# Queue order at stage borders, preparation transfers on GpSimd's queue, and a state-space stage written in a fixed order

## The chip, the cores and the metric

The kernel runs on one core of a Trainium2 chip. The metric is the device time of one execution in microseconds; the time shown for a kernel is the median of its runs. The core has TensorE (PE, matrix products; PEld are its weight loads), VectorE (DVE), ScalarE (ACT), GpSimd (POOL) and SyncE (SP). Each engine executes its instructions in the order in which they stand in its program; transfers (DMA) are issued from a queue of SP, ACT or POOL, and the issue itself waits its turn in that engine's program.

## What is computed

One decoding step of two layers for 512 prompt and 64 sample positions (576 columns together), all in float32:

```python
# layer 0: gated spatial MLP and differential attention, one output projection, then a SwiGLU feed-forward
a   = up * spatial_gate(vp, sgu_w, sgu_b)
b   = diff_head_out(diff_attn(q, k, v, lam), subln)
x1  = x  + concat(a, b) @ w_out_even
x2  = x1 + (silu(gate) * up) @ w_ffn_out          # gate, up = split(rmsnorm(x1) @ w_ffn_in), 22 blocks of 128
# layer 1: S5, 64 groups of 16 channels, one complex state of 64 each
s   = associative_scan(a_bar, b_bar @ rmsnorm(x2)) + a_cum * s0
y   = Re(c @ s) + d * u
z   = gelu(y) @ w_glu + b_glu
x3  = x2 + z[:, :1024] * sigmoid(z[:, 1024:])
x4  = x3 + swiglu(rmsnorm(x3))
out = rmsnorm(x4)                                  # and the new cache rows and the last states
```

## The kernel before

Activations are kept transposed, 128 channels by 576 columns, eight such tiles for the 1024 channels. A float32 product is made of three products in a shorter format: the weight is split into `wh` (a cast on ACT, L260) and `wl` (the rest, on DVE, L263), the activation into `hi` (ACT, L227 or L230) and `lo` (DVE, L228 or L231), and PE adds hi·wh, lo·wh and hi·wl (L278), 288 columns at a time. A *unit* is one output tile of 128 channels: `Stream` loads the raw weight (L245, on SP's queue, two buffers that hold two units each), splits it at most two units ahead, and runs `unit_mm` (L269), either half of the columns after the other, or, where `kmajor` is set, k by k with both halves in turn. Each half ends in an `evac` on DVE.

The stages in order of time: input projection; attention with side work; the output projection into `x1` (`ev_o`, L1040); feed-forward 0 (`push_ffn`, in four parts of 6, 6, 6 and 4 blocks, each with its gate and up units and then eight down units); the S5 stage; the gated units (`ev_z1`); feed-forward 1; the last norm. `s5_prep` (L1256 on) works beside feed-forward 0 in small portions: for every k of 0 to 7 (eight groups each) it makes the matrices Gk, Fk and Tk of the state-space model with DVE, ACT and PE, stores them to scratch tensors in DRAM (dG, dF, and dZ from which dL is copied with a shift), and the S5 stage loads them back (`s5_load`, L1563).

A norm needs the sum of squares over 1024 channels. `Stat.add` (L985) squares each new tile on ACT (L987, L990), adds it into `acc` on POOL (L998), and `mm` (L1001) sums `acc` and the last square over the partitions on PE (`ssq`, L1007).

For each k the S5 stage does: U scaled by the norm (L1639, DVE), `vp` = U·Gk (L1645, PE), rotation, W and scan on DVE (L1666, L1667, L1682, L1683), a second rotation and the states `X` (L1692, DVE), `yp` = Tk·U + Fk·X (L1702, L1708, PE), copies on ACT, transposes (L1722, PE), gelu and split. The letters of `SORD` give the order in which the functions for k, k+1 and so on are called.

What sets the order: a scheduler orders the instructions of each engine with estimates of its own, except where the text pins them (`keep`) or, in the changed kernel, inside `tc.manual_schedule()`, where the program's order stands. Small tiles come from rings: 44 buffers for `blk`, 19 for `ablk`, 5 in the pool `op`; four PSUM banks each for `mbank` and `bank`.

## Time and profile before

| | us |
|---|---|
| median of 3 runs | 1432.93 (1428.97 to 1440.73) |
| the profiled execution | 1436.56 |
| its span, first to last instruction | 1434.86 |
| mean granted TensorE clock | 0.986 |
| PE busy | 1384.8 |

The difference of execution and span, 1.7 us, lies outside the instructions. PE is busy 97% of the span; the rest is to be read as stretches in which PE has nothing to do, and besides these there are stretches in which its clock was granted at half. The trace shows two levels, 1.0 (2.4 GHz) and 0.5 (1.2 GHz).

### The profile page before, as it was taken

How to read it: one execution, taken by the hardware profiler on the slowest of the kernel's cores; microseconds unless marked ns; L12 is line 12 of the kernel's file. 1: busy time of each engine (PE TensorE's matmuls, PEld its weight loads, DVE VectorE, ACT ScalarE, POOL GpSimd, SP SyncE). 2: the span in 40 equal slices, each digit the busy share in tenths (PEclk: the TensorE clock that was granted, in tenths of full speed). 3: DMA queues.
4: the chain of work that ended last, by engine and by line, in shares of the span. 5: the costliest groups of instructions: out<-in, count | busy, mean ns of one | idle time of the engine just before them, and what ended most of it. 6: DMA issues, size and time to landing. Idle time of an engine off the chain costs nothing. (4 is left out here: it accounts for less than half of the span.)

```text
span 1434.9 us, 27625 instructions
## 1 busy us (share of the span) xinstructions
PE 1384.8 (97%) x11382; PEld 1317.7 (92%) x11382; DVE 840.3 (59%) x1979; ACT 482.8 (34%) x866; POOL 182.3 (13%) x220
## 2 busy tenths in 40 slices
PE   7999999989999999999999979999999999999997
PEld 6888887769999999999998968999999999999997
DVE  5544567567599545987964487544444444444455
ACT  4233465433332123333322535433221221222234
POOL 2453553431000000000000200010000000000002
PEclk9999999999999999999999979999999999999999
DMA  8565653453322433555456684233223322322411
GB/s 240 166 199 179 202 178 104 133 180 122 89 80 87 133 89 80 152 145 147 146 141 179 201 238 134 68 89 89 62 72 103 89 74 74 89 81 75 110 59 67
DMA packets 223557, 177.37 MB, mean 124 GB/s; under 512 B 34060, under 2 KB 199752, under 8 KB 223432
## 3 DMA queue, kind: packets, MB, share of 16 engines
q1 hardware_dynamic: 206312, 136.01, 32.9%
q0 software_dynamic: 10880, 35.66, 8.2%
q10 hardware_dynamic: 6240, 3.93, 0.9%
q8 instruction: 90, 1.47, 0.4%
q14 instruction: 35, 0.29, 0.1%
HBM read 154.24 MB, written 25.53 MB: 125 GB/s over the span
## 5 line engine op out<-in xcount | busy, mean ns | idle before, releaser
L278 PE MATMUL acc<-hi,wh 128*128 128x288 f32 x2432 | 724.3, 298 | 6.0 <-ACT wh L260 3.1
L278 PE MATMUL acc<-hi,wl 128*128 128x288 f32 x2432 | 720.1, 296 | 1.5 <-DVE wl L263 1.5
L278 PE MATMUL acc<-lo,wh 128*128 128x288 f32 x2432 | 719.4, 296 | 0.0
L278 PEld LDWEIGHTS acc<-hi,wh 128*128 128x128 f32 x2432 | 458.7, 189 | 12.6 <-ACT hi L227 4.5
L278 PEld LDWEIGHTS acc<-hi,wl 128*128 128x128 f32 x2432 | 458.9, 189 | 3.7 <-DVE wl L263 2.4
L278 PEld LDWEIGHTS acc<-lo,wh 128*128 128x128 f32 x2432 | 459.1, 189 | 0.9 <-issue 0.8
L260 ACT CAST wh<-raw 128x1024 fp32r<-128x1024 f32 (+2 forms) x196 | 185.0, 945 | 592.9 <-PE acc L278 410.8
L263 DVE TENSOR_TENSOR wl<-raw,wh 128x1024 fp32r<-128x1024 f32 (+2 forms) x195 | 214.1, 1099 | 56.1 <-ACT wh L260 54.4
L1121 DVE TENSOR_TENSOR tu<-acc,rb 128x288 f32<-128x288 f32 x88 | 40.1, 455 | 124.6 <-PE acc L278 124.5
L278 PE MATMUL acc<-gxh,wh 128*128 128x288 f32 x320 | 100.2, 316 | 0.9 <-DVE proj L372 0.9
L1111 DVE TENSOR_TENSOR tg<-acc,rb 128x288 f32<-128x288 f32 x88 | 39.9, 455 | 97.1 <-PE acc L278 96.1
L278 PE MATMUL acc<-gxl,wh 128*128 128x288 f32 x320 | 96.4, 302 | 0.0
L278 PE MATMUL acc<-gxh,wl 128*128 128x288 f32 x320 | 95.5, 301 | 0.6 <-DVE wl L263 0.6
L998 POOL TENSOR_TENSOR acc<-acc,sq 128x576 f32<-128x576 f32 x18 | 26.8, 1488 | 480.9 <-ACT sq L990 480.9
L1131 DVE TENSOR_TENSOR x<-acc,x 128x288 f32<-128x288 f32 x96 | 43.6, 456 | 73.5 <-PE acc L278 73.1
L731 POOL DMA_INDIRECT pg<-in_cache_v_dram,pidx x64 | 65.0, 1016 | 82.9 <-PE so L853 49.4
L731 POOL DMA_INDIRECT pg<-in_cache_k_dram,pidx x64 | 64.1, 1001 | 71.8 <-PE ktp L786 36.4
L278 PEld LDWEIGHTS acc<-gxh,wh 128*128 128x128 f32 x320 | 60.9, 191 | 8.7 <-issue 8.0
L1841 POOL TENSOR_TENSOR sq<-sq,sq 128x288 f32<-128x288 f32 x12 | 9.6, 802 | 431.2 <-ACT sq L1837 431.2
L278 PEld LDWEIGHTS acc<-gxh,wl 128*128 128x128 f32 x320 | 60.7, 190 | 1.7 <-DVE wl L263 0.8
L278 PEld LDWEIGHTS acc<-gxl,wh 128*128 128x128 f32 x320 | 61.1, 191 | 1.0 <-issue 0.7
L227 ACT CAST hi<-tu 128x576 fp32r<-128x576 f32 x44 | 29.8, 677 | 41.9 <-DVE tu L1123 41.9
(441 smaller groups left out, 1474.0 us busy)
## 6 DMA issues: line engine op xcount, KB each, us to landing
raw<-in_w_ffn_in_dram SPq DMA_DIRECT2D x88, 512.0 KB
raw<-in_w_ffn_out_dram SPq DMA_DIRECT2D x24, 768.0 KB
raw<-in_w_in_even_dram SPq DMA_DIRECT2D x10, 1024.0 KB
...
```

The costliest lines, as they stand in the source:

```text
L227: A.copy(hi, src)
L260: c = A.copy(hi[:, 0:nk], src)
L263: c = (lo_eng or V).tensor_tensor(lo[:, 0:nk], src, f32(hi[:, 0:nk]), op=ALU.subtract)
L278: PE.matmul(pts[hf], lhsT=w[:, k, :], rhs=x[:, c0:c1], start=(k == 0 and wi == 0), stop=(k == nk - 1 and wi == 2))
L731: G.indirect_dma_start(out=t, out_offset=None, in_=src, in_offset=bass.IndirectOffsetOnAxis(ap=pidx[:, 8 * b + j:8 * b + j + 1], axis=0))
L998: G.tensor_tensor(self.acc[:, 0:NT], self.acc[:, 0:NT], q, op=ALU.add)
L1111: V.tensor_tensor(half(t, hf), pt, half(stat.need(), hf), op=ALU.mult)
L1121: V.tensor_tensor(half(t, hf), pt, half(stat.need(), hf), op=ALU.mult)
L1131: V.tensor_tensor(half(nxt[m], hf), pt, half(cur[m], hf), op=ALU.add)
L1841: G.tensor_tensor(acc[h], acc[h], q, op=ALU.add)
```

## The change

- `Stat.add` adds on DVE instead of POOL, and the `ssq` matmuls of `acc` move from the last `add` to the start of `steps`, which the driver calls later. In `ev_o` and `ev_z1` the split of a tile stands before its `add`, so ACT makes `hi` before the square.
- In `push_ffn` the first down unit of a part runs k by k.
- All transfers of `s5_prep` move to POOL's queue: those of ACT (ast, s0st, zz, dq) and those of SP (braw, cst, dF, dG, dZ, dL). dF gets another layout: two stores of 256 pieces of 512 B a half, and two loads of 128 partitions instead of four of 64.
- `s5_load` of k = 0 and 1 goes to POOL's queue too; the tables come out of the pool `op`; the order is Gk, tables, Tk, Fk.
- The S5 stage stands in `tc.manual_schedule()`, in the order 'LVDrxsRcoyg'. Both `vp` are in `bank`. X is written 64 wide and the last state copied out by ACT (L1694 goes); both W additions come before the two scans; two gated units instead of one run inside the stage.

```diff
-SORD = 'LrxsRVDcyog'
+SORD = 'LVDrxsRcoyg'
...
-        def add(self, x, pre=True):
+        def add(self, x):
...
-                    if pre:
-                        self.mm(self.acc, True)
...
-                    G.tensor_tensor(self.acc[:, 0:NT], self.acc[:, 0:NT], q, op=ALU.add)
+                    V.tensor_tensor(self.acc[:, 0:NT], self.acc[:, 0:NT], q, op=ALU.add)
...
         def steps(self):
             yield
+            self.mm(self.acc, True)
             r = self.tm()
...
+            gx1[m] = split(x1[m], g_ffn0[:, m:m + 1])
             st1.add(x1[m])
-            gx1[m] = split(x1[m], g_ffn0[:, m:m + 1])
...
-                    W.push(loads[mp], nf, hs, [ev(2 * mp), ev(2 * mp + 1)])
+                    W.push(loads[mp], nf, hs, [ev(2 * mp), ev(2 * mp + 1)], kmajor=(mp == 0))
...
-    dF = [dp.tile([P, 8, P], F32, name=f"dF{k}") for k in range(KD)]
+    dF = [dp.tile([2, 64, 2, 512], F32, name=f"dF{k}") for k in range(KD)]
...
-                SP.dma_start(out=br[64 * c:64 * c + 64], in_=I[key][0, 32 * hf:32 * hf + 32].rearrange("g p c -> p g c"))
+                G.dma_start(out=br[64 * c:64 * c + 64], in_=I[key][0, 32 * hf:32 * hf + 32].rearrange("g p c -> p g c"))
...
-                SP.dma_start(out=dL[k].rearrange("(c t) g n -> t c g n", t=8)[t],
+                G.dma_start(out=dL[k].rearrange("(c t) g n -> t c g n", t=8)[t],
                              in_=dZ[k][:, :, 16 * (7 - t):16 * (7 - t) + P].rearrange("g c n -> c g n"))
...
     def s5_load(k):
+        Q = G if k < 2 else SP
...
-        vp = [mbank("vp"), bank("vp")]
+        vp = [bank("vp"), bank("vp")]
...
-            V.tensor_tensor(x2k[k][:, c, :, 1:64], t1[:, c, :, 0:63], t2[:, 1 - c, :, 0:63], op=ALU.subtract if c == 0 else ALU.add)
-        for c in range(2):
-            V.tensor_tensor(fin2[:, c, 4 * k:4 * k + 4], t1[:, c, :, 63], t2[:, 1 - c, :, 63], op=ALU.subtract if c == 0 else ALU.add)
+            V.tensor_tensor(x2k[k][:, c, :, 1:65], t1[:, c], t2[:, 1 - c], op=ALU.subtract if c == 0 else ALU.add)
+        A.copy(fin2[:, :, 4 * k:4 * k + 4], x2k[k][:, :, :, 64])
+        A.copy(x2k[k][:, :, :, 64:72], s0[:, :, 4 * k:4 * k + 4, :])
...
-    glu0 = unit_mm(u0["hl"], u0["xs"], u0["nk"], u0["evac"], True, 1)
+    glus = [unit_mm(u["hl"], u["xs"], u["nk"], u["evac"], True, 1) for u in W.q[W.done:W.done + 2]]
...
-    for i in range(KD + 4):
-        for c in SORD:
-            f, d = steps[c]
-            on(f, i + d)
+    with tc.manual_schedule():
+        ru_mm(st2.last, False)
+        ru = rstd_fast(ru["ps"][:, 0:NCH], NCH, DM)
+        for k in range(VA):
+            on(s5_v, k)
+        on(s5_d0, 0)
+        for i in range(KD + 3):
+            for c in SORD:
+                f, d = steps[c]
+                on(f, i + d)
```

First place, the end of the output projection. DVE before: the two halves of `x1`, the next weight's rest, and the tile's `lo`, once per unit.

```order
L1047 TENSOR_TENSOR x_4626<-acc_4613,xa_4265 128x36x8
L1047 TENSOR_TENSOR x_4626<-acc_4628,xa_4265 128x36x8
L263 TENSOR_TENSOR wl_4650<-raw_4527,wh_4649 128x512
L231 SCALAR_TENSOR_TENSOR lo_4646<-x_4626,gvec,hi_4645 128x576
L1047 TENSOR_TENSOR x_4666<-acc_4653,xa_4333 128x36x8
L1047 TENSOR_TENSOR x_4666<-acc_4668,xa_4333 128x36x8
```

DVE after, the same tiles (the names' numbers differ a little, and so do the lines):

```order
L1046 TENSOR_TENSOR x_4626<-acc_4613,xa_4265 128x36x8
L1046 TENSOR_TENSOR x_4626<-acc_4628,xa_4265 128x36x8
L263 TENSOR_TENSOR wl_4650<-raw_4527,wh_4649 128x512
L231 SCALAR_TENSOR_TENSOR lo_4643<-x_4626,gvec,hi_4642 128x576
L996 TENSOR_TENSOR acc_316<-acc_316,sq_4646 128x576
L1046 TENSOR_TENSOR x_4666<-acc_4653,xa_4333 128x36x8
L1046 TENSOR_TENSOR x_4666<-acc_4668,xa_4333 128x36x8
```

The addition into `acc` has come onto DVE as a fifth instruction per tile, behind `lo`. PE at the same place, before, from the last matmul of the output projection on (acc_4704) into the first gate unit (acc_4791):

```order
L278 MATMUL acc_4704<-hi_3238,wl_4650 128x288
L1004 MATMUL ssq_4720<-ones 64x1
L1007 MATMUL ssq_4720<-ones,acc_316 128x1
L1007 MATMUL ssq_4720<-ones,acc_316 64x1
L1007 MATMUL ssq_4720<-ones,acc_316 128x1 x3
L278 MATMUL acc_4791<-hi_4441,wh_4783 128x288
```

PE after, where `ssq` stands now (acc_4784 and acc_4788 are the halves of the first gate unit, hi_4562 its fourth k):

```order
L278 MATMUL acc_4784<-hi_4562,wl_4777 128x288
L278 MATMUL acc_4788<-hi_4562,wh_4776 128x288
L278 MATMUL acc_4788<-lo_4563,wh_4776 128x288
L278 MATMUL acc_4788<-hi_4562,wl_4777 128x288
L1002 MATMUL ssq_4810<-ones 64x1
L1005 MATMUL ssq_4810<-ones,acc_316 128x1
L1005 MATMUL ssq_4810<-ones,acc_316 64x1
L1005 MATMUL ssq_4810<-ones,acc_316 128x1 x3
```

The sum over `acc` has moved behind the first four k, that is 24 matmuls, of the gate unit.

Second place, the gate and up units of the last part of feed-forward 0. ACT before (tg is a gate, hi_9453 the split of a block whose `tu` DVE makes; raw_9269 is the weight of the next two units):

```order
L1113 ACTIVATE tg_9240<-tg_9240 128x576
L260 CAST wh_9334<-raw_9134 128x1024
L227 CAST hi_9330<-tu_9301 128x576
L1113 ACTIVATE tg_9363<-tg_9363 128x576
L227 CAST hi_9453<-tu_9424 128x576
L260 CAST wh_9395<-raw_9269 128x1024
L260 CAST wh_9489<-raw_9269 128x1024
L260 CAST wh_9549<-raw_9392 128x1024
```

ACT after, the same place (raw_9285 is that weight):

```order
L1112 ACTIVATE tg_9240<-tg_9240 128x576
L260 CAST wh_9350<-raw_9119 128x1024
L227 CAST hi_9346<-tu_9317 128x576
L260 CAST wh_9411<-raw_9285 128x1024
L1112 ACTIVATE tg_9379<-tg_9379 128x576
L260 CAST wh_9473<-raw_9285 128x1024
L227 CAST hi_9469<-tu_9440 128x576
L260 CAST wh_9561<-raw_9408 128x1024
```

The casts of that weight have moved ahead of the block's gate and split: one before each. SP's queue there, before (dL and dG are stores of the preparation, raw_9269 and raw_9392 weights):

```order
L245 DMA raw_9134<-in_w_ffn_in_dram 128x8x128 x2
L1448 DMA dG_4738<-gt_9185 128x512
L1452 DMA dL_4761<-dZ_4753 16x8x128 x8
L1452 DMA dL_4762<-dZ_4754 16x8x128 x8
L245 DMA raw_9269<-in_w_ffn_in_dram 128x8x128 x2
L245 DMA raw_9392<-in_w_ffn_in_dram 128x8x128 x2
```

SP's queue after, the same weights and what follows (the loads of k = 2 and then the second down weight, raw_9681):

```order
L245 DMA raw_9119<-in_w_ffn_in_dram 128x8x128 x2
L245 DMA raw_9285<-in_w_ffn_in_dram 128x8x128 x2
L245 DMA raw_9408<-in_w_ffn_in_dram 128x8x128 x2
L245 DMA raw_9559<-in_w_ffn_out_dram 128x4x256
L1570 DMA Gk_10149<-dG_4726 128x512
L1570 DMA Gk_10150<-dG_4726 128x512
L1577 DMA tabk_10155<-dT_4757 128x512
L1577 DMA tabk_10157<-dT_4757 128x512
L1570 DMA Tk_10159<-dL_4750 128x512
L1570 DMA Tk_10160<-dL_4750 128x512
L1581 DMA Fk_10153<-dF_4734 128x512
L245 DMA raw_9681<-in_w_ffn_out_dram 128x4x256
```

The 17 stores between the weights are gone from SP; the loads of k = 2 stand ahead of raw_9681 and wait there for POOL's stores.

## Rows read from the trace of the kernel before

**Rows 1.** The page: busy time of the engines over the span.

```profile
PE 1384.8 (97%) x11382; PEld 1317.7 (92%) x11382; DVE 840.3 (59%) x1979; ACT 482.8 (34%) x866; POOL 182.3 (13%) x220
```

**Rows 2.** The waits of PE over the whole span: total us, times, longest.

```profile
PE vp L1645 <- DMA Gk<-dG: 3.4, 4, 1.8
PE yp L1708 <- DVE X L1692: 3.4, 1, 3.4
PE acc L278 <- ACT wh L260: 3.1, 1, 3.1
...
PE vp L1645 <- DVE U L1639: 2.8, 1, 2.8
...
PE acc L278 <- ACT hi L227: 2.5, 1, 2.5
PE ssq L1007 <- POOL acc L998: 2.5, 1, 2.5
...
PE ru L1525 <- POOL X L1657: 0.4, 1, 0.4
```

**Rows 3.** Busy time by stretch (start:end in us): length, then PE, PEld, DVE, ACT and POOL busy with their instructions, the granted clock, the share of the DMA engines and GB/s.

```profile
337.00:352.00 15.00, 14.97 (x113) 14.74 (x112) 11.02 (x15) 8.29 (x13) 4.22 (x3) 1.00 0.22 73
352.00:362.00 10.00, 8.98 (x62) 7.98 (x60) 8.20 (x12) 4.15 (x6) 2.93 (x3) 1.00 0.56 159
362.00:365.00 3.00, 0.53 (x5) 0.50 (x5) 2.63 (x4) 2.28 (x3) 1.74 (x6) 0.99 0.55 137
364.90:371.80 6.90, 6.90 (x31) 6.88 (x32) 3.11 (x5) 1.36 (x2) 0.00 (x0) 0.51 0.52 145
450.00:453.70 3.70, 1.15 (x9) 0.92 (x8) 3.70 (x14) 0.67 (x1) 0.00 (x0) 1.00 0.18 71
453.70:457.10 3.40, 3.40 (x16) 3.40 (x16) 2.57 (x8) 0.00 (x0) 0.00 (x0) 0.50 0.70 229
766.00:771.10 5.10, 1.57 (x11) 1.11 (x10) 3.26 (x5) 2.57 (x3) 0.00 (x0) 1.00 1.03 326
771.10:774.50 3.40, 3.40 (x14) 3.40 (x15) 1.07 (x1) 0.00 (x0) 0.00 (x0) 0.50 1.04 261
829.20:836.00 6.80, 5.23 (x88) 5.23 (x90) 6.37 (x12) 1.25 (x4) 0.15 (x2) 0.50 0.99 252
842.80:846.20 3.40, 3.40 (x48) 3.08 (x46) 3.33 (x9) 1.58 (x5) 0.00 (x0) 0.50 0.31 91
853.10:859.90 6.80, 6.20 (x47) 5.43 (x48) 5.55 (x11) 2.33 (x7) 0.15 (x2) 0.50 0.72 215
```

**Rows 4.** DVE in order of time, one unit at the end of the output projection: start, length, instruction, and in brackets the idle time before it and what ended that.

```profile
352.60 1.28 DVE L1047 TENSOR_TENSOR x<-acc,xa 128x288 f32<-128x288 f32 x2
353.70 0.70 DVE L263 TENSOR_TENSOR wl<-raw,wh 128x512 fp32r<-128x512 f32 x1
355.30 1.49 DVE L231 SCALAR_TENSOR_TENSOR lo<-x,gvec,hi 128x576 fp32r<-128x576 f32 x1 [0.90 <-ACT hi L230]
356.71 1.30 DVE L1047 TENSOR_TENSOR x<-acc,xa 128x288 f32<-128x288 f32 x2
```

**Rows 5.** The last `lo` of that stage on DVE, and ACT in order of time for one tile.

```profile
367.62 0.82 DVE L231 SCALAR_TENSOR_TENSOR lo<-x,gvec,hi 128x576 fp32r<-128x576 f32 x1 [0.43 <-ACT hi L230]
...
358.05 0.68 ACT L990 ACTIVATE sq<-x 128x576 f32<-128x576 f32 x1 [2.27 <-DVE x L1047]
358.64 0.76 ACT L230 ACTIVATE hi<-x,gvec 128x576 fp32r<-128x576 f32 x1
```

**Rows 6.** Groups of instructions: DVE's product of two 128 by 576 float32 tiles in the S5 stage, and POOL's addition into `acc` (count, busy us, mean ns, idle before and its releaser).

```profile
L1639 DVE TENSOR_TENSOR U<-U,rsr 128x576 f32<-128x576 f32 x8 | 5.7, 750 | 0.4 <-DMA U<-dU 0.3
...
L998 POOL TENSOR_TENSOR acc<-acc,sq 128x576 f32<-128x576 f32 x18 | 26.8, 1488 | 480.9 <-ACT sq L990 480.9
```

**Rows 7.** ACT in order of time at the stall of 766 us.

```profile
768.16 0.67 ACT L227 CAST hi<-tu 128x576 fp32r<-128x576 f32 x1 [6.53 <-DVE tu L1123]
768.74 1.04 ACT L260 CAST wh<-raw 128x1024 fp32r<-128x1024 f32 x1
```

**Rows 8.** DVE and ACT in order of time in the S5 stage: the first `X` on DVE, and ACT at the end of the stage.

```profile
841.18 0.75 DVE L1692 TENSOR_TENSOR X<-rt,rt 128x252 f32<-128x252 f32 x2
...
897.47 1.28 ACT L1616 ACT_TABLE_LOAD   x1
898.88 0.89 ACT L1616 ACTIVATE z<-acc,gvec 128x288 f32<-128x288 f32 x2
```

**Rows 9.** Transfers issued by POOL, as groups, and the stretch in which the eight stores to dT were issued (columns as in rows 3).

```profile
L731 POOL DMA_INDIRECT pg<-in_cache_v_dram,pidx x64 | 65.0, 1016 | 82.9 <-PE so L853 49.4 <-PE ktp L786 20.1 <-issue 8.5
...
L1376 POOL DMA_DIRECT2D dT<-tab x8 | 4.4, 552 | 62.4 <-DVE ct L1246 36.9 <-DVE tab L1251 14.9 <-DVE tab L1250 9.8
...
447.00:478.00 31.00, 28.45 (x204) 28.22 (x203) 29.14 (x131) 5.68 (x7) 4.40 (x8) 0.94 0.38 128
```

**Rows 10.** The two loads of braw on SP's queue and the first reads of it on DVE; the last bias addition `kr` of k = 3 and the first read of braw for k = 4.

```profile
558.33 3.12 SPq L1381 DMA_DIRECT2D braw<-in_ssm_b_im_dram  x1
...
564.53 0.22 DVE L1474 TENSOR_SCALAR pk<-braw 64x128 f32<-64x128 f32 x1 [0.84 <-DMA braw<-in_ssm_b_im_dram]
...
644.78 0.18 DVE L1437 TENSOR_TENSOR kr<-kr,dq 128x32 f32<-128x32 f32 x1
...
660.74 0.22 DVE L1475 COPY pk<-braw 64x128 f32<-64x128 f32 x1
```

More of the change, by code (lines that the diff above doesn't have):

```diff
@@ L1264, in s5_prep @@
         for c, key in enumerate(("state_ssm_re", "state_ssm_im")):
-            A.dma_start(out=s0st[:, :, 64 * c:64 * c + 64],
+            G.dma_start(out=s0st[:, :, 64 * c:64 * c + 64],
                         in_=I[key][0].rearrange("b g p -> (b g) p").rearrange("(i r) p -> r i p", r=P))
@@ L1269, in s5_prep @@
         for k in range(KD):
-            A.dma_start(out=dZ[k].rearrange("g c n -> (g c) n")[:, 0:112], in_=zz)
+            G.dma_start(out=dZ[k].rearrange("g c n -> (g c) n")[:, 0:112], in_=zz)
         yield
@@ L1389, in s5_prep @@
         for q in range(4):
-            A.dma_start(out=dq[32 * q:32 * q + 32],
+            G.dma_start(out=dq[32 * q:32 * q + 32],
                         in_=I["ssm_d"][0].rearrange("(k par pr c) -> pr k par c", k=8, par=2, pr=4)[q].partition_broadcast(32))
@@ L1438, in kernel_rows @@
             for q in range(4):
-                SP.dma_start(out=dZ[k].rearrange("(par pr) c n -> pr c par n", par=2)[q][:, :, 112:240], in_=kr[32 * q:32 * q + 16])
+                G.dma_start(out=dZ[k].rearrange("(par pr) c n -> pr c par n", par=2)[q][:, :, 112:240], in_=kr[32 * q:32 * q + 16])
             ready.append(k)
@@ L1496, in s5_prep @@
                 f = outer(Cx, Cy, gs, js, 9, PU[0], PU[1], "Fn")
-                SP.dma_start(out=dF[k][:, js, :], in_=f[:, :, 1:9, :].rearrange("p g d c -> p g (d c)"))
+                for c in range(2):
+                    G.dma_start(out=dF[k][hh, :, c].rearrange("p (g n) -> p g n", g=4),
+                                 in_=f[64 * c:64 * c + 64, :, 1:9, :].rearrange("p g d c -> p g (d c)"))
                 late.append((kernel_rows, (k, hh, f, Bx)))
@@ L1534, in ev_x2 @@
             return
-        st2.add(n, False)
+        st2.add(n)
         if m == KD - 1:
@@ L1566, in pair @@
             for hf in range(2):
-                SP.dma_start(out=ts[hf], in_=src[:, 4 * hf:4 * hf + 4, :])
+                Q.dma_start(out=ts[hf], in_=src[:, 4 * hf:4 * hf + 4, :])
             return ts
@@ L1570, in s5_load @@
         fk = [ablk("Fk", (P, 4, P)) for _ in range(2)]
-        for c in range(2):
-            for pa in range(2):
-                SP.dma_start(out=fk[c][64 * pa:64 * pa + 64], in_=dF[k][64 * c:64 * c + 64, 4 * pa:4 * pa + 4, :])
-        tk = pair(dL[k], "Tk")
         if k % 2 == 0:
             for c in range(2):
-                t = ablk("tabk", (P, 8, 64))
-                SP.dma_start(out=t.rearrange("p a n -> p (a n)"), in_=dT[k // 2][:, c, :])
+                t = op.tile([P, 8, 64], F32, tag="op", name=nm("tabk"))
+                Q.dma_start(out=t.rearrange("p a n -> p (a n)"), in_=dT[k // 2][:, c, :])
                 tabs[k // 2, c] = t
+        tk = pair(dL[k], "Tk")
+        for c in range(2):
+            Q.dma_start(out=fk[c].rearrange("p j n -> p (j n)"), in_=dF[k].rearrange("pa p c n -> (pa p) c n")[:, c, :])
         par[k] = (gk, fk, tk)
@@ L1595 @@
         return
-    ru_mm(st2.last, False)
-    ru = rstd_fast(ru["ps"][:, 0:NCH], NCH, DM)
     fin = const("fin", [P, 64])
@@ L1626, in f @@
             V.tensor_tensor(x3[m], x2[m], zs.pop(m), op=ALU.add)
+            gx3[m] = split(x3[m], g_ffn1[:, m:m + 1])
             st3.add(x3[m])
-            gx3[m] = split(x3[m], g_ffn1[:, m:m + 1])
         return f
@@ L1657, in s5_d0 @@
         G.memset(x2k[k][:, :, :, 0:1], 0.0)
-        A.copy(x2k[k][:, :, :, 64:72], s0[:, :, 4 * k:4 * k + 4, :])
     def s5_rot(k, src):
@@ L1682, in s5_scan @@
             V.tensor_tensor(w[:, c], t1[:, c], t2[:, 1 - c], op=ALU.add if c == 0 else ALU.subtract)
+        for c in range(2):
             V.tensor_tensor_scan(z[:, c].rearrange("p a n -> p (a n)"), d, w[:, c].rearrange("p a n -> p (a n)"),
@@ L1691, in s5_x @@
         for c in range(2):
-            V.tensor_tensor(x2k[k][:, c, :, 1:64], t1[:, c, :, 0:63], t2[:, 1 - c, :, 0:63], op=ALU.subtract if c == 0 else ALU.add)
-        for c in range(2):
-            V.tensor_tensor(fin2[:, c, 4 * k:4 * k + 4], t1[:, c, :, 63], t2[:, 1 - c, :, 63], op=ALU.subtract if c == 0 else ALU.add)
+            V.tensor_tensor(x2k[k][:, c, :, 1:65], t1[:, c], t2[:, 1 - c], op=ALU.subtract if c == 0 else ALU.add)
+        A.copy(fin2[:, :, 4 * k:4 * k + 4], x2k[k][:, :, :, 64])
+        A.copy(x2k[k][:, :, :, 64:72], s0[:, :, 4 * k:4 * k + 4, :])
     def s5_y(k):
@@ L1713, in s5_y @@
             for hf in range(2):
-                A.copy(ys[hf][:, :, 4 * jh:4 * jh + 4, :], src[:, 4 * hf:4 * hf + 4])
+                E = V.tensor_copy if k == KD - 1 and jh else A.copy
+                E(ys[hf][:, :, 4 * jh:4 * jh + 4, :], src[:, 4 * hf:4 * hf + 4])
     def s5_out(k):
@@ L1728, with glu @@
     W.prefetch()
-    u0 = W.q[W.done]
-    glu0 = unit_mm(u0["hl"], u0["xs"], u0["nk"], u0["evac"], True, 1)
+    glus = [unit_mm(u["hl"], u["xs"], u["nk"], u["evac"], True, 1) for u in W.q[W.done:W.done + 2]]
+    def glu(k):
+        for g in glus:
+            next(g)
+            if k == KD - 1:
+                next(g, None)
     def on(f, k):
@@ L1736 @@
     steps = dict(L=(s5_load, 2), V=(s5_v, VA), D=(s5_d0, 1), r=(s5_rot1, 0), R=(s5_rot2, 0), s=(s5_scan, 0), x=(s5_x, -1),
-                 c=(s5_vs, 0), y=(s5_y, -1), o=(s5_out, -2), g=(lambda k: next(glu0), -3))
-    for k in range(VA):
-        on(s5_v, k)
-    on(s5_d0, 0)
-    for i in range(KD + 4):
-        for c in SORD:
-            f, d = steps[c]
-            on(f, i + d)
-    for _ in glu0:
-        pass
-    W.done += 1
+                 c=(s5_vs, 0), y=(s5_y, -1), o=(s5_out, -2), g=(glu, -3))
+    with tc.manual_schedule():
[8 more added lines that the diff above has]
+                on(f, i + d)
+    W.done += 2
     def states_out():
```

10 lines of the change are left out of this document (5 added, 5 removed).

## The prediction

> **What bounds the kernel now.** First the page's busy times: PE works 1384.8 us of 1434.9, every other engine at most 59% [rows 1]. So only time that PE loses counts, and it loses it by waiting, and by running at the half level of its clock. Second the waits of PE, to see which are touched: six of 2.5 to 3.4 us and one of 0.4, all but one of them single events at a border between stages [rows 2]. Third the windows around each, for the clock: a stretch at 0.5 follows every one of these gaps of 2.5 us or more, and there the same matmuls take about twice as long [rows 3].
>
> I count a border's loss in matmuls. Undisturbed, PE does 113 in 15.0 us, 0.1327 us each [rows 3]. At the first border it does 62 where 75.4 fit, then 5 of 22.6, then, at half clock, 31 of 52.0: 52 missing, 6.9 us. At 450 us 9 of 27.9 and 16 of 25.6: 3.8 us. At 766 us 11 of 38.4 and 14 of 25.6: 5.2 us. In the S5 stage the kinds of matmul differ, so I add waits and clock: 3.4 + 3.4 + 2.8 of waits [rows 2], and half of what PE was busy in the three half-clock stretches, (5.23 + 3.40 + 6.20) / 2 = 7.4 [rows 3]; 17.0 together. All that the change can reach is so 33.3 us with the 0.4.
>
> **First border (352 to 372 us).** DVE sets the pace here: one unit's two x to the next takes 356.71 - 352.60 = 4.11 us [rows 4], while PE needs 24 x 0.1327 = 3.18. In the 4.11 stand 0.90 of waiting for `hi`, because ACT squares (0.68) before it scales (0.76) [rows 5], and a `lo` of 1.49; the one `lo` at which POOL was not adding took 0.82 [rows 4, 5]. After: x to wl 1.10; wl 0.60 to the next start and about 0.3 of waiting, since `hi` now ends 0.76 after x; lo 0.72; and the new addition, which no row shows on DVE. Its bounds are the 0.75 of a product of the same shape on DVE and the 1.49 on POOL [rows 6]; I take 0.75, the row of the engine, 0.66 to the next start. That is 3.4 us, 0.2 over PE instead of 0.93, and PE's lead, which in 337 to 352 covered some units of the larger deficit, covers this. At 1.49 it would be 4.1, as now.
> The 2.5 us of `ssq` waiting for POOL go, because 24 matmuls (3.18 us) stand ahead of it now. What is late next is the last square: x ends about 1.0 us after PE's last matmul, `hi` takes 0.76, the square 0.68: 2.4 us, still under 3.18. I leave 0.5 us of loss: **gain 6.4**, between 4.0 (pace as now, only the wait and part of the clock) and 6.9. The other additions, 18 in all [rows 6], cost DVE 13.5 us in stages where it has room (59%), so nothing there.
>
> **450 us.** PE waits 2.5 us for `hi` of the last block [rows 2], behind DVE, which is busy all 3.70 us of that window [rows 3]. k by k, the last block is wanted after 30 matmuls instead of 15: 2.0 us later. About 0.55 remains, too short to be followed by half clock as far as these rows go. **Gain 3.2**, between 0 (DVE's preparation pieces fill the room) and 3.8.
>
> **766 us.** The cast that PE waits for stood on ACT behind `hi` of a block, which itself waited 6.53 us for DVE's product and so for PE [rows 7]. That order is gone: one cast stands before each gate and each split, as in the undisturbed units, since the weight no longer follows 17 stores on SP. **Gain 5.2**, between 2 (the weight lands late) and 5.2.
>
> **Before S5.** The 0.4 wait of `ru` goes, 0 to 0.4.
>
> **S5 stage.** Unchanged: the first `vp` waits 2.8 for U, and the half-clock stretch after it (5.23 / 2 = 2.6). What changes:
> - The Gk waits (3.4 in four): Gk is first in each group of loads, k = 0 to 2 are there before the stage. I take 2.9 back. The half clock at 853 to 860, which follows the longest of them, goes: 3.1.
> - The first X starts at 841.18 [rows 8]. Two U products of 0.68 to the next start that are now behind the first rotation (all five stood ahead) bring it forward about 1.2; that much less waiting. But `vp` of k = 2 and `yp` of k = 0 now stand behind the third U, and PE does them at half clock: 2.0 lost.
> - Two gated units end together. Then ACT loads its table and does two sigmoids (0.89 each, 0.75 to the next start) before the next cast of 1.04 [rows 7, 8]; before, the second unit's matmuls lay over that. 2 x 0.75 + 1.04 = 2.5, less what the table load hides: I take 2.4 lost; with half clock behind it 4, at best 0.5.
> Together 2.9 + 3.1 + 1.2 - 2.0 - 2.4 = **gain 2.8**, between -3 (the last two larger, loads late in each k) and +10 (17.0 less what is unchanged and 1.6).
>
> **The preparation on POOL's queue.** Per k it issues 18 transfers: 4 dF, 2 dG, 4 dZ, 8 dL. POOL's rows give 0.55 us (stores of dT) and 1.02 (gathers) [rows 9]. dL must wait until dZ has landed; the load of braw was read 3.1 us after its issue of 3.12 ended, so about 3.1 [rows 10]. A k comes every (660.74 - 564.53) / 4 = 24.1 us [rows 10]. POOL needs 18 x 0.55 + 3.1 = 13.0, at 1.02 21.5: both fit, cost 0. The loads of braw are unlike the others, 2048 pieces of 64 B each; on SP one took 3.12 [rows 10], and 16 stores of 128 pieces at 0.55 would be 8.8. The second pair stands between `kr` of k = 3 and its first use 16.0 us later [rows 10], with five other transfers: 5 x 0.55 + 2 x 3.12 + 3.1 = 12.1, hidden; with 8.8 each 23.5, 7.5 late. I take SP's, the same transfer, and keep 7.5 for the range.
> While the dT stores were issued, DVE was busy 29.1 of 31.0 us, and each took 0.55 all the same [rows 9].
> The Trainium skill ("SBUF — State Buffer", section "SBUF: two separate sides") warns that a transfer from GpSimd's queue has its descriptors written by GpSimd's cores, which a DVE copy or cast in a two-port mode locks out, so that the transfer stands still, and advises the SP or ACT queue. By that rule this part would lose, and more the busier DVE is. By the row it costs nothing, and the sum goes by the row.
>
> **Sum.** 6.4 + 3.2 + 5.2 + 0.4 + 2.8 = 18.0. From the profiled execution of 1436.56 that is 1418.6, from the median of 1432.93, 3.6 lower, 1414.9. The runs shown lie 11.8 us apart, so neither base is better: **1417**. A difference under 1%, 14.3 us, is about what a measurement of this kernel can't tell from none: faster is below 1418.6, slower above 1447.3.
>
> **Rivals.**
> *The gains come in part* (0.25). DVE's pace stays near 4 us at the first border, the stretch after 450 stays DVE's, and S5 gives back at its end: 4.0 + 0 + 5.2 + 0.4 - 3 = 6.6, between 1426 and 1430, so 1428. For it: DVE is full at 450 [rows 3]; the addition's price is not shown. Against it: the 0.90 of waiting for `hi` is plainly the order of ACT [rows 4, 5].
> *The change does at 766 only half of what it says* (0.10): the order is right, the weight comes late, since the windows show 326 GB/s there [rows 3]: the gain there is 2, 1420.
> *POOL's queue falls behind* (0.10), the other side. Its 18 transfers of a k pass 24.1 us from 1.17 us each on. At 1.6 us a k takes 31.9, 7.8 too long, 62 after eight; DVE then waits for the buffers of Fn and Gn, which POOL's stores free, after about one k of delay (24.1): 38 us of stall at DVE, and PE waits for DVE: 1417 + 38 = 1455. From about 1.55 it is slower than before by over 1%. The loads of k = 2 on SP, which stand ahead of the second down weight and wait for those stores, would show it too. For it: dL's and dF's pieces are smaller than dT's, and no row shows POOL issuing 18 in a row. Against it: 0.55 and 1.02.
> The case of that page of the Trainium skill is this one with another cause of the price; its chance is in the 0.10.
>
> **The numbers.** Forecast 0.55, rivals 0.25, 0.10, 0.10. Faster by over 1%: 0.85 of the forecast's 0.55 and a little of the second rival, 0.48. Slower: the POOL rival, 0.10. Same: the rest, 0.42. Range: the upper bounds, 6.9 + 3.8 + 5.2 + 0.4 + 10 = 26.3 from the median, 1407; the lower ones give 4.0 + 0 + 2 + 0 - 3 = 3.0 from the profiled execution, 1433.6, and with a part of braw's 7.5, 1436. The forecast's own range is 1409 to 1423.
>
> **What would show it.** Right: no wait of PE for `ssq` and no half clock at 365; x pairs about 3.4 us apart; the wait for `hi` at 450 near 0.5; no wait for `wh` at 766; waits for Gk under 1 us; one new wait of PE for `wh` or `wl` behind the S5 stage, 2 to 3 us. Wrong: the addition on DVE well over 0.75; POOL transfers over 1 us, or DVE waiting for dF or braw; PE waiting for the loads of each k.

## The result: 1.4% faster, and where the 20.6 us come from

The changed kernel took 1415.05 us (median of 4 runs, 1413.23 to 1418.70) against 1435.70 for the kernel before on the same chip: ratio 0.9864, 95% interval 0.9832 to 0.9897. In a second comparison it took 1416.15 against 1436.52, ratio 0.9856 [0.9831, 0.9881]. The forecast was 1417 from 1432.93, that is 0.9889, and the measured ratio lies just past the 1% that was to tell faster from no change. (The median of before moved from 1432.93 to 1435.70 with a fourth run.)

These are the busy times on the page of the changed kernel, to be held against [rows 1]. GpSimd works 79.5 us more, the others about the same; PE works 12.8 us less on the same matmuls.

```profile
PE 1372.0 (97%) x11382; PEld 1308.1 (93%) x11382; DVE 841.7 (60%) x1983; ACT 484.8 (34%) x872; POOL 261.8 (19%) x387
```

These are the waits of PE in the changed kernel over the span (total us, times, longest), to be held against [rows 2]. Of the seven there, `ssq`, `wh` at 766, the first `X`, the four for Gk and `ru` are gone, and `hi` at 450 is down from 2.5 to 1.0. One wait of 2.8 stays and one of 4.6 is new, both under "issue" (the trace has no releaser for them; they are the `vp` of k = 0 and of k = 2). A wait of 1.5 for `ys` is new too, and the 0.7 for `wh` now stands behind the S5 stage.

```profile
PE vp L1645 <- issue: 7.4, 2, 4.6
...
PE vp L1645 <- ACT ys L1715: 1.5, 1, 1.5
...
PE acc L278 <- DVE wl L263: 1.2, 3, 0.6
PE acc L278 <- ACT hi L227: 1.0, 1, 1.0
...
PE acc L278 <- ACT wh L260: 0.7, 1, 0.7
PE acc L278 <- DVE lo L228: 0.7, 2, 0.4
```

The windows of the changed kernel follow (columns as in [rows 3]). At the first border PE does 73 and 78 matmuls in 10 us each, no clock below 1.00; at 443.5 it misses 13 of 30; the stretch of 30 us in which the late weight had stopped it is full; the S5 stage still has its half clock.

```profile
352.00:362.00 10.00, 9.60 (x73) 9.35 (x71) 9.67 (x15) 5.60 (x9) 0.00 (x0) 1.00 0.46 127
362.00:372.00 10.00, 10.00 (x78) 9.59 (x77) 5.87 (x18) 3.85 (x7) 0.00 (x0) 1.00 0.38 107
443.50:447.50 4.00, 2.60 (x17) 2.15 (x17) 4.00 (x10) 1.35 (x2) 0.00 (x0) 1.00 0.24 67
740.00:770.00 30.00, 30.00 (x228) 30.00 (x228) 14.08 (x20) 8.46 (x10) 6.44 (x13) 1.00 0.75 246
809.00:818.00 9.00, 3.60 (x66) 3.34 (x65) 6.17 (x14) 2.85 (x9) 0.36 (x4) 0.81 0.92 238
818.00:824.80 6.80, 4.79 (x45) 4.68 (x46) 6.77 (x13) 1.59 (x6) 0.15 (x2) 0.50 0.77 258
```

Single executions differ by several us ahead of the first border, where the edits change nothing of weight: the matmul that opens the first column of the table below starts at 345.7 us in one trace of the changed kernel, at 348.9 in another, and at 352.5 in e6_ssq_early. So totals of single runs can't be split. The stages can: every kernel here issues the same 8448 matmuls of L278, and I took the time from the start of the n-th to the start of a later one in each profiled trace. The numbers are us; the S5 column holds the whole S5 stage with the first gated units on both sides of it.

```
                 output proj.  450      preparation  766       S5 stage
from-to          1250-1392     1920-2016 2016-4032   4032-4320 4320-4800
before             30.3         17.1      288.5       43.8      132.2
changed            23.2         14.7      286.8       38.2      127.5
  difference       -7.1         -2.4       -1.8       -5.6       -4.7
e1_border          23.2         17.1      289.1       43.5      130.1
e2_kmajor          28.8         14.6      287.6       43.2      130.0
e3_poolq           28.8         17.3      288.9       38.2      125.9
e4_s5              28.8         17.1      288.5       43.8      129.4
e5_acc_pool        24.1         14.9      286.2       38.2      127.2
e6_ssq_early       26.9         14.7      286.9       38.2      127.5
e10_old_s5         23.2         14.7      286.6       38.2      124.2
e7_u_early         23.1         14.7      286.9       38.2      123.3
e8_u_gelu          24.7         14.7      286.6       38.2      123.3
```

The five differences add up to 21.6 us; the spans differ by 23.4, the medians by 20.6. The profile of before was unlucky in two places that its code does not explain: the other kernels with the old border took 28.8 there, and those with the old stage and old loads 130. In both places its clock was at half for longer: 6.8 us behind the border against 3.4 in e2, e3 and e4, and 17.0 us in the S5 stage against 13.6 in e1 and 10.2 in e2. Read so, the border gives 5.6 and the S5 stage 2.5 to 4.7, and a difference of 1.5 us between single profiles can be one such stretch of 3.4 us.

### The profile page after: what moved, and what is told of

It is laid out like the page before. It is cut to its first block, busy times and chain, and to the rows that moved or that the text cites. A ratio compares the mean times of both kernels' runs of the same rounds, so it can differ in the third digit from the quotient of the medians.

```text
span 1411.5 us, 27626 instructions
## 1 busy us (share of the span) xinstructions
PE 1372.0 (97%) x11382; PEld 1308.1 (93%) x11382; DVE 841.7 (60%) x1983; ACT 484.8 (34%) x872; POOL 261.8 (19%) x387
## 4 chain that ended last, share of the span: by engine, by line
PE 87%; DVE 7%; DMA 3%; issue 2%; ACT 1%; SPq 1%; POOL 0%; POOLq 0%; ACTq 0%; DVEq 0%
PE acc L278 72%; PE ktp L786 2%; DMA pg<-in_cache_v_dram,pidx 1%; PE ssc L767 1%; PE S L632 1%; DVE wl L263 1%; PE yp L1702 1%; PE so L853 1%; PE yp L1708 1%; PE vp L1645 1%; PE O L665 1%; DMA xt<-in_x_sample_dram 1%; PE gT L1444 1%; PE satp L827 1%; DVE x L1046 0%
## 5 line engine op out<-in xcount | busy, mean ns | idle before, releaser
L278 PE MATMUL acc<-hi,wh 128*128 128x288 f32 x2432 | 722.1, 297 | 1.9 <-ACT hi L227 1.0
L278 PE MATMUL acc<-lo,wh 128*128 128x288 f32 x2432 | 717.2, 295 | 0.7 <-DVE lo L228 0.7
L278 PE MATMUL acc<-hi,wl 128*128 128x288 f32 x2432 | 717.1, 295 | 0.6 <-DVE wl L263 0.6
L278 PEld LDWEIGHTS acc<-hi,wh 128*128 128x128 f32 x2432 | 456.4, 188 | 9.0 <-issue 5.9
L278 PEld LDWEIGHTS acc<-lo,wh 128*128 128x128 f32 x2432 | 456.6, 188 | 2.3 <-DVE lo L228 1.2
L278 PEld LDWEIGHTS acc<-hi,wl 128*128 128x128 f32 x2432 | 456.5, 188 | 1.8 <-DVE wl L263 1.0
L278 PE MATMUL acc<-gxh,wh 128*128 128x288 f32 x320 | 100.3, 317 | 0.9 <-DVE proj L372 0.9
L278 PE MATMUL acc<-gxl,wh 128*128 128x288 f32 x320 | 96.4, 302 | 0.0
L278 PE MATMUL acc<-gxh,wl 128*128 128x288 f32 x320 | 95.5, 301 | 0.6 <-DVE wl L263 0.6
L278 PEld LDWEIGHTS acc<-gxh,wh 128*128 128x128 f32 x320 | 60.9, 191 | 8.7 <-issue 8.0
L278 PEld LDWEIGHTS acc<-gxh,wl 128*128 128x128 f32 x320 | 60.7, 190 | 1.7 <-DVE wl L263 0.8
L278 PEld LDWEIGHTS acc<-gxl,wh 128*128 128x128 f32 x320 | 61.2, 192 | 1.0 <-issue 0.7
L1497 POOL DMA_DIRECT2D dF<-Fn x32 | 20.0, 631 | 129.8 <-DVE Fn L1418 129.8
L791 DVE COPY kt<-ktp 128x512 f32<-128x512 f32 x32 | 22.0, 688 | 34.3 <-PE ktp L786 34.2
```

The costliest lines, as they stand in the source:

```text
L278: PE.matmul(pts[hf], lhsT=w[:, k, :], rhs=x[:, c0:c1], start=(k == 0 and wi == 0), stop=(k == nk - 1 and wi == 2))
L791: V.tensor_copy(kt, tp)
L1497: G.dma_start(out=dF[k][hh, :, c].rearrange("p (g n) -> p g n", g=4), in_=f[64 * c:64 * c + 64, :, 1:9, :].rearrange("p g d c -> p g (d c)"))
```

## The experiments

**The four parts, each alone.** The first takes only the lines on the norm.

```diff
-                    G.tensor_tensor(self.acc[:, 0:NT], self.acc[:, 0:NT], q, op=ALU.add)
+                    V.tensor_tensor(self.acc[:, 0:NT], self.acc[:, 0:NT], q, op=ALU.add)
...
+            self.mm(self.acc, True)
             r = self.tm()
...
+            gx1[m] = split(x1[m], g_ffn0[:, m:m + 1])
             st1.add(x1[m])
-            gx1[m] = split(x1[m], g_ffn0[:, m:m + 1])
```

> The kernel before with the norm's part of the change alone: the sum of squares added on VectorE, the split ahead of the add, the ssq matmuls later. Theory (the first border's 6.9 us are lost there and nowhere else): no wait of PE for ssq, no half clock after 362 us, x pairs 3.5 to 3.6 us apart instead of 4.11; 6.4 to 6.9 us less, and the losses at 450 (2.5 us wait, 3.8 in all), 766 (3.1 and 0.5) and in the S5 stage stand as before. Rival (the preparation beside it sets the pace, so a border reached earlier waits longer at the next one): the wait at 450 grows to 4 us or more and the sum is 4 us or less.

Measured 1429.04 us (one run; before on the same chip 1435.67). The border took 23.2 us as in the changed kernel, PE's only wait there was 0.4 for `wl`, and 450 and 766 stand as before. The theory holds: the loss was local and is not handed on. Of the 7.1 us, 1.5 is the luck of the profile of before.

The second is the one argument in `push_ffn`.

```diff
-                    W.push(loads[mp], nf, hs, [ev(2 * mp), ev(2 * mp + 1)])
+                    W.push(loads[mp], nf, hs, [ev(2 * mp), ev(2 * mp + 1)], kmajor=(mp == 0))
```

> The kernel before with the first down unit of each part run k by k, alone. Theory: the wait for hi at 450 shrinks by 15 matmuls, 2.0 us, from 2.5 to about 0.5, and the 3.4 us at half clock go: 3.2 to 3.8 us less, the other borders as before. Rival (VectorE's preparation pieces fill the room, as it was busy all of that window): hi comes later as well, the wait stays over 1.5 us, 1 us less or nothing.

Measured 1428.98. The 450 column falls by 2.5 us, the half clock there is gone, and these are what is left of the wait (waits of PE from 440 to 470 us):

```profile
PE acc L278 <- ACT hi L227: 0.9, 1, 0.9
PE acc L278 <- DVE lo L228: 0.4, 1, 0.4
```

Between the two expectations and nearer the theory: 1.3 us remain instead of 0.5, since after `hi` PE waits for `lo` too.

The third moves the preparation's transfers and the loads of k = 0 and 1, with dF's new layout and the new order of the loads, and changes neither border nor stage.

```diff
-                SP.dma_start(out=dL[k].rearrange("(c t) g n -> t c g n", t=8)[t],
+                G.dma_start(out=dL[k].rearrange("(c t) g n -> t c g n", t=8)[t],
...
     def s5_load(k):
+        Q = G if k < 2 else SP
```

> The kernel before with the preparation's transfers and the loads of k = 0 and 1 on GpSimd's queue, the new layout of dF and the new order of the loads, nothing else. Theory: the casts of the late weight stand ahead of the gate and split again, the waits of 3.1 and 0.5 us at 766 and the half clock behind them go, 5.2 us less; a transfer costs GpSimd 0.55 to 0.65 us and nobody waits for the queue; the preparation itself takes as long as before; the S5 stage's waits for Gk go in part because k = 0 to 2 are there (up to 3 us more). Rival (the queue falls behind, or only the order of the casts matters and the loads now collide with weights elsewhere): a wait of VectorE for dF, dZ or braw, or new waits of PE for wh between 560 and 760 of together 3 us or more.

Measured 1424.68. The 766 column falls by 5.6 us, to the very 38.2 of the changed kernel, and the S5 stage by 6.3 (4.1 against the 130 of e1 and e2). That is the theory. But the sign that the rival named stands in this run too: VectorE waits for braw and dF, and PE for `cst` (waits from 350 to 780 us).

```profile
DVE pk L1475 <- DMA braw<-in_ssm_b_re_dram: 4.7, 1, 4.7
DVE ft L1417 <- DMA dF<-Fn: 2.2, 1, 2.2
PE cT L1473 <- DMA cst<-in_ssm_c_im_dram: 1.7, 1, 1.7
```

GpSimd's program in order of time shows why braw was late: its load stood behind a dL store that waited until dZ had landed.

```profile
649.21 0.55 POOL L1452 DMA_DIRECT2D dL<-dZ  x1 [3.58 <-DMA dZ<-kr]
649.75 1.11 POOL L1381 DMA_DIRECT2D braw<-in_ssm_b_re_dram  x1
```

The preparation column is 288.9 all the same, against 288.5 before, so these waits hardly lengthened it. Which of this run's three edits (queue, layout, order of the loads) gave the S5 stage its 4 to 6 us was not taken apart.

The groups of GpSimd's transfers in the changed kernel (count, busy us, mean ns, idle before and its releaser) show the price that the sum took:

```profile
L1451 POOL DMA_DIRECT2D dL<-dZ x64 | 34.3, 540 | 14.7 <-DMA dZ<-kr 10.7 <-issue 4.0
L1497 POOL DMA_DIRECT2D dF<-Fn x32 | 20.0, 631 | 129.8 <-DVE Fn L1418 129.8
L1438 POOL DMA_DIRECT2D dZ<-kr x32 | 16.3, 515 | 19.0 <-DVE kr L1436 19.0
...
L1447 POOL DMA_DIRECT2D dG<-gt x16 | 9.1, 572 | 20.6 <-ACT gt L1446 20.5
...
L1380 POOL DMA_DIRECT2D braw<-in_ssm_b_re_dram x2 | 2.2, 1123 | 0.0
```

That is 0.52 to 0.63 us each, and 1.1 for the 2048 small pieces of braw, while VectorE was busy for 144.4 of the 174 us from 566 to 740. In the changed kernel the queue waits for VectorE far more than the other way round: from 350 to 760 us VectorE's only wait for a transfer is 0.5 us, and PE's is 0.8, for `cst`.

```profile
DVE pk L1473 <- DMA braw<-in_ssm_b_im_dram: 0.5, 1, 0.5
```

The fourth is the S5 stage alone, on the old loads.

```diff
-SORD = 'LrxsRVDcyog'
+SORD = 'LVDrxsRcoyg'
...
+    with tc.manual_schedule():
```

> The kernel before with the S5 stage in its fixed order and two gated units in it; the loads stay on SyncE's queue in their old order. Theory (the order of the stage is what counts): the first X waits for nobody, one wait of about 4.5 us for the third U stands in its place, the Gk waits are under 1 us since each group's Gk is asked for a whole iteration ahead; from the first vp to the end of the second gated unit 4 to 6 us less, the rest as before. Rival (the stage gains because k = 0 to 2 were loaded early and over GpSimd's queue): the Gk waits stay at 2 us or more and the stage gains 2 us or less.

Measured 1435.19. The stage took 129.4: 2.8 less than the profile of before, 0.7 less than e1 and e2. The signs are the theory's: no wait for the first X, one of 4.0 for the third U, and only 0.7 for Gk although the loads stayed on SyncE's queue. The 4 to 6 us are not there: in time the rival is nearer, though its Gk waits of 2 us or more are not there either. PE's waits only moved: they are 10.2 us in all in this stage (2.8, 4.0, 1.5 for a later U, 0.7, and 1.2 at its end), against 9.3 in e1. On the old loads the order is worth 0.7 us (2.8 against the profile of before); the loads alone gave 4.1 to 6.3 (e3).

**Is the order of the stage worth anything on the new loads?** The changed kernel with the whole stage of before put back:

```diff
-SORD = 'LVDrxsRcoyg'
+SORD = 'LrxsRVDcyog'
...
-    with tc.manual_schedule():
+    ru_mm(st2.last, False)
+    ru = rstd_fast(ru["ps"][:, 0:NCH], NCH, DM)
```

> The changed kernel with the S5 stage of the kernel before (scheduler's order, one gated unit in it, vp in both bank pools), the loads and everything else as changed. Theory from the two parts run alone (the loads gave the stage about 6 us, the fixed order at most 3, both together 5.6): from the first vp to the end of the second gated unit the same time as in the changed kernel, within 1 us; one wait for X of about 2 us stands for the wait of 4.6 us for the third U. Rival (the fixed order has its worth only with the early loads): 3 us longer or more.

Measured 1411.42, and the stage 124.2, 3.3 us *less* than in the changed kernel. Neither the theory (within 1 us) nor the rival: on the new loads the fixed stage costs time. How much is less sure: e3 had the same old stage on the same loads and took 125.9, 1.6 less than the changed kernel. The clock was at half for 6.8 us in e10's stage and for 10.2 in e3's and in the changed kernel's, so, at the 1.5 that such a stretch of 3.4 us cost above, about half of the 3.3 is that. PE's waits in that stage, with the old order on the new loads:

```profile
PE vp L1647 <- DVE U L1641: 2.8, 1, 2.8
PE yp L1710 <- issue: 2.1, 1, 2.1
PE vp L1647 <- DMA Gk<-dG: 1.5, 2, 0.8
```

**Why it costs.** PE in the changed kernel, in order of time (start, length, instruction, idle before): both first `vp`, then a wait of 4.58 and, around its end, a half-clock stretch in which the 16 matmuls of `yp` take 3.27 instead of 1.91 (their time in the next k).

```profile
811.98 3.45 PE L1645 MATMUL vp<-U,Gk 128*64 128x72 f32 x64 [2.83 <-issue]
820.01 2.19 PE L1645 MATMUL vp<-U,Gk 128*64 128x72 f32 x32 [4.58 <-issue]
822.12 3.27 PE L1702 MATMUL yp<-Tk,U 128*72 128x128 f32 x16
825.33 1.97 PE L1708 MATMUL yp<-Fk,X 64*72 64x128 f32 x32
```

VectorE at the same time: the third U starts at 819.15, behind rotation, W, scan and rotation of k = 0, and X of k = 0 behind the first rotation of k = 1.

```profile
817.94 0.69 DVE L1665 TENSOR_TENSOR rt<-Zt,tabk 128x512 f32<-128x512 f32 x1
...
819.15 0.75 DVE L1639 TENSOR_TENSOR U<-U,rsr 128x576 f32<-128x576 f32 x1
819.83 0.68 DVE L1665 TENSOR_TENSOR rt<-Vt,tabk 128x512 f32<-128x512 f32 x1
820.43 0.68 DVE L1666 TENSOR_TENSOR rt<-Vt,tabk 128x512 f32<-128x512 f32 x1
821.03 0.75 DVE L1692 TENSOR_TENSOR X<-rt,rt 128x256 f32<-128x256 f32 x2
```

So the next kernel scales U ahead and puts X first:

```diff
-SORD = 'LVDrxsRcoyg'
+SORD = 'LVDxrsRUcoyg'
...
+    def s5_u(k):
+        V.tensor_tensor(U[k], U[k], ru.unsqueeze(1).to_broadcast([P, 8, NCH]), op=ALU.mult)
...
+    steps = dict(L=(s5_load, 2), U=(s5_u, 3), V=(s5_v, VA),
...
+        for k in range(3):
+            on(s5_u, k)
```

> The changed kernel with VectorE's order in the S5 stage altered: U of k = 0 to 2 scaled at once, later ones three k ahead, and X of k-1 before the first rotation of k. Theory (VectorE's place of the third U makes PE's wait of 4.6 us, and X stands behind a rotation that nobody wants yet): the wait at the third vp goes, one of 1 to 2.5 us for X comes in its place, the half clock of 6.8 us that follows goes or is halved; 3 to 5 us less in the stage. Rival (the chain of VectorE to the first X is the limit and the wait only moves): a wait for X of 4 us or more, 1 us less or nothing.

Measured 1411.31; the stage 123.3, 4.2 less than in the changed kernel. The two groups do not overlap: 123.3 in all three profiles with this order (e7, e8, e11), 127.2 to 127.6 in the four with the old one (the changed kernel, e5, e6, e12). PE does all three first `vp` without a break, and waits 1.31 for X, as the theory had it.

```profile
814.24 6.00 PE L1647 MATMUL vp<-U,Gk 128*64 128x72 f32 x96 [2.83 <-issue]
820.16 1.97 PE L1704 MATMUL yp<-Tk,U 128*72 128x128 f32 x16
823.45 1.97 PE L1710 MATMUL yp<-Fk,X 64*72 64x128 f32 x32 [1.31 <-ACT X L1696]
```

The half clock is not gone, though, only down from 10.2 us to 6.8: from 813.3 to 820.1, around the end of the 2.83 that stays, and now the `vp` run in it.

One more line was to take out the wait of 1.5 us behind ScalarE's table load:

```diff
+        A.activation(epst[:, 1:2], epst[:, 0:1], AF.Gelu_apprx_tanh)
```

> As e7_u_early, and ScalarE loads the table of its gelu right after the norm's square root, while it waits for the first vp, instead of before the first gelu. Theory: the wait of 1.5 us for the copies ys, which stand behind that table load of 1.28 us, goes: 1 to 1.5 us less than e7_u_early. Rival: ScalarE's copies are late for another reason (they queue behind the gelu and its cast), nothing less.

Measured 1412.01, the stage 123.3: nothing gained. In e7 the wait for `ys` was already 0.6. In e8 it is gone, and PE waits for X instead, 1.6 and 1.0 (1.3 once in e7). The rival's "nothing less" holds; its reason, copies behind the gelu and its cast, is not shown. With U early it is X that PE wants last.

**The first border: which of its three edits counts?** The changed kernel with the addition back on GpSimd:

```diff
-                    V.tensor_tensor(self.acc[:, 0:NT], self.acc[:, 0:NT], q, op=ALU.add)
+                    G.tensor_tensor(self.acc[:, 0:NT], self.acc[:, 0:NT], q, op=ALU.add)
```

> The changed kernel with one line back: the sum of squares added on GpSimd again (acc += sq), everything else as changed. Theory A (what set VectorE's pace at the first border was the wait for hi, that is ScalarE's order, and lo slowed by GpSimd's addition beside it): hi now ends first, so lo runs before the square is there and takes 0.8 us, GpSimd adds under the next x, the pace falls to PE's 3.2 us, nobody waits for ssq, and the border costs no more than in the changed kernel, 0 to 0.4 us less. Theory B (moving the addition to VectorE is itself what counts): lo takes 1.4 to 1.5 us again, the pace goes back to 4 us and PE waits 2 us or more at ssq.

Measured 1417.68. VectorE in order of time: `lo` takes 0.82 with GpSimd adding again, and a unit takes 3.16 and 3.19 us (350.44 to 353.60 to 356.79), PE's own 3.18.

```profile
350.44 1.58 DVE L1046 TENSOR_TENSOR x<-acc,xa 128x288 f32<-128x288 f32 x2
351.85 0.69 DVE L263 TENSOR_TENSOR wl<-raw,wh 128x512 fp32r<-128x512 f32 x1
352.86 0.82 DVE L231 SCALAR_TENSOR_TENSOR lo<-x,gvec,hi 128x576 fp32r<-128x576 f32 x1 [0.33 <-ACT hi L230]
353.60 1.61 DVE L1046 TENSOR_TENSOR x<-acc,xa 128x288 f32<-128x288 f32 x2
```

In the changed kernel, with the addition on VectorE, the pace is 3.58:

```profile
345.87 1.33 DVE L1046 TENSOR_TENSOR x<-acc,xa 128x288 f32<-128x288 f32 x2
347.00 0.72 DVE L263 TENSOR_TENSOR wl<-raw,wh 128x512 fp32r<-128x512 f32 x1
348.05 0.82 DVE L231 SCALAR_TENSOR_TENSOR lo<-x,gvec,hi 128x576 fp32r<-128x576 f32 x1 [0.33 <-ACT hi L230]
348.78 0.75 DVE L996 TENSOR_TENSOR acc<-acc,sq 128x576 f32<-128x576 f32 x1
349.45 1.31 DVE L1046 TENSOR_TENSOR x<-acc,xa 128x288 f32<-128x288 f32 x2
```

Theory A: with the split ahead of the square, GpSimd could have kept the addition. No wait at `ssq` came back. That the split sets the pace follows by elimination, since the later `ssq` gives VectorE nothing else to do; no run put the square of the changed kernel back first. The table's 24.1 against 23.2 goes with a stretch of 3.4 us at half clock, which came with no gap ahead of it (below) and stands in runs without this edit as well.

The changed kernel with the `ssq` matmuls back at the last add:

```diff
                     self.last = q
+                    if not self.fast:
+                        self.mm(self.acc, True)
...
             yield
-            self.mm(self.acc, True)
             r = self.tm()
```

> The changed kernel with the ssq matmuls of acc issued again from the last add, that is at the end of the output projection instead of behind four k of the gate unit. Prediction's reading (the wait went because 24 matmuls stand ahead): PE waits 1.5 to 2.5 us at ssq again. Rival (the wait went because VectorE, done sooner, has acc ready before PE's last matmul of the projection): no wait over 0.3 us, the time as in the changed kernel.

Measured 1423.95. One wait, between the two expectations:

```profile
PE ssq L1007 <- DVE acc L998: 0.9, 1, 0.9
```

So of the 2.5 us [rows 2] about 1.6 went because `acc` is ready sooner, and 0.9 because 24 matmuls stand ahead. Behind that wait this run had 6.8 us at half clock; with the 0.9 they make its border 26.9, 3.7 longer. Whether the wait caused them is open, since four runs without it (e5, e8, e11, e12) had half as much.

**How near was GpSimd's queue to its limit?** The changed kernel with each dL store in four:

```diff
+DLP = 4
...
+                for q in range(DLP):
+                    cs = slice(16 // DLP * q, 16 // DLP * (q + 1))
```

> The changed kernel with each store to dL in four pieces of 32 rows instead of one of 128: 42 transfers a k on GpSimd's queue instead of 18, the bytes the same. If a transfer costs about 0.55 us whatever its size: 42 x 0.55 + 3 = 26 us a k against 24, the queue ends its stores 15 to 25 us later, the loads of k = 0 and 1 with it, VectorE begins to wait for dF or dZ, and the time is 0 to 5 us longer. If the cost goes by the rows of a transfer (128 rows 0.54, so 32 rows under 0.25): nothing is later, the time as in the changed kernel.

Measured 1515.48, 100 us longer, which neither expectation had. Views of that run tell how. Its group of the dL stores (count, busy us, mean ns, idle before):

```profile
L1454 POOL DMA_DIRECT2D dL<-dZ x256 | 155.9, 617 | 12.4 <-issue 3.7 <-DMA dL<-dZ 3.5 <-DMA dZ<-kr 2.6
```

GpSimd's longest wait from 660 to 770 us:

```profile
POOL dF L1500 <- DVE Fn L1419: 88.7, 1, 88.7
```

And PE's longest wait from 540 to 920 us:

```profile
PE ru L1529 <- POOL win L1547: 64.6, 1, 64.6
```

The price goes by the transfer, not by its rows: 0.62 us for 32 rows, 0.54 for 128. The queue did fall behind: the load of braw for k = 4 was issued at 670.3 us instead of 640.4. But it was not simply full: after that it stood idle for 88.7 us waiting for VectorE, whose part of the preparation for k = 4 stood far back in VectorE's program (the loads of braw were issued by 672.5 us, and VectorE first read it at 757, waiting for PE and not for braw in between). What is late then is paid by an instruction that has nothing to do with the stores: the fill of `win` stands behind them in GpSimd's program, and PE waits 64.6 us for it.

```profile
867.07 26.66 POOL L1454 DMA_DIRECT2D dL<-dZ  x44 [0.86 <-issue]
902.94 0.13 POOL L1547 MEMSET win<- 128x17 f32 x1
```

Another 24.4 us of PE's waits are for VectorE's pieces of the preparation (13.3 at `gT`, 11.1 at `kp`, against 0.8 in the changed kernel). So the 100 us come in good part from the order that the scheduler made of the longer program, and the path of the prediction's slow rival does not show: VectorE did not wait for a buffer that a store held. At how many transfers the queue alone costs time the run doesn't tell.

**The better version, timed.** e7_u_early again, and the changed kernel beside it.

> e7_u_early again, timed. Theory (its S5 stage is 4 us shorter, the rest is the changed kernel): 4 us less than the changed kernel on the same chip, about 1411, ratio to the kernel before 0.982 to 0.985. Rival (the 4 us in one profile are the scatter of single runs): within 1.5 us of the changed kernel.

> The changed kernel timed again beside e11_best: ratio to the kernel before 0.985 to 0.988, about 1415.

Measured 1414.21 (5 runs, 1412.33 to 1415.54), ratio to before 0.9843 [0.9818, 0.9868], and 1416.15 (6 runs, 1413.11 to 1419.62), 0.9856 [0.9831, 0.9881]. The stage is 4.3 us shorter in the profiles of these runs as well (123.3 and 127.6). The totals differ by 1.9 us in the mean, with 2.5 either way (from the scatter of the 5 and 6 runs): between the two expectations, and the totals alone do not settle it.

## Why the prediction was right, step by step

The total was 18.0 us forecast and 20.6 measured. The two borders and 766 came out as reasoned; that the whole came so near is in part luck, since the S5 term was made of parts that were wrong in both directions, and 1.8 us came from a stage that the sum left out. Of its terms:

- **First border, 6.4:** 7.1 against the profile of before, on which the forecast was worked out, and 5.6 against e2, e3 and e4, whose half-clock stretch was 3.4 us and not 6.8. The mechanism (ScalarE's order sets VectorE's pace) follows from e5. The price of the addition on VectorE was right, 0.75. The pace came out at 3.58 rather than 3.4, since the wait for `hi` is 0.33 and `wl` to `lo` takes 1.05 in all, and PE's lead covered it all the same: one wait of 0.40 was left, as the 0.5 said. The reason given for `ssq` was only a third of it (e6: 0.9 of 2.5 us).
- **450 us, 3.2:** 2.4. I counted the wait for `hi`, which came to 1.0 instead of 0.55, and forgot that PE wants `lo` after it, another 0.4.
- **766 us, 5.2:** 5.6, and e3 shows that moving the transfers and loads brings it, without the other three parts.
- **Before S5, 0.4:** gone in the changed kernel, and back (0.4) in e5, where GpSimd adds again.
- **GpSimd's queue, nothing:** 0.52 to 0.63 us a transfer, braw 1.1 instead of the 3.12 taken. Nothing is right for the changed kernel; e3 shows that it was near, with VectorE waiting 4.7 us for braw. There the wait came from the order on the queue and not from the price. The Trainium skill's warning ("SBUF — State Buffer", section "SBUF: two separate sides") would have these transfers stand still beside VectorE copies or casts in a two-port mode. No run here shows it: the price stayed at 0.52 to 0.63, and e3 took as long for the preparation as the kernel before. But the warning was hardly put to the test: of VectorE's instructions from 566 to 740 us in the changed kernel 215 are TENSOR_TENSOR, and the 28 COPY and TENSOR_SCALAR take 6.6 us together; the 18 transfers that ran beside one of those took 0.51 to 0.58. While the dT stores of [rows 9] were issued, VectorE ran TENSOR_TENSOR alone.
- **The preparation, not in the sum:** 1.8 us less. e2 shows 0.9 of it, e3 none; I have no experiment for the rest.
- **S5, 2.8:** 4.7 against the profile of before. Right in its sign, wrong in its parts. The gain is the loads': no wait for Gk is left (0.5 was priced). The first X gave all of its 3.4 us of waiting, not 1.2. The end stall of 2.4 was 0.7 + 0.3 + 0.2. And the step that `vp` of k = 2 and `yp` of k = 0 would lose 2.0 behind the third U named the right place at less than half its price: 4.58 of wait, with a half-clock stretch of 6.8 around its end. The half clock was priced at half of PE's busy time; [rows 3] give about 0.4 (31 matmuls where 52 fit). The fixed stage as a whole is a loss of 1.6 to 3.3 (e3, e10), which the early loads covered.
